# A hybrid decoder layer: two U steps moved ahead of the gate stage, and v loaded four blocks ahead

## The chip, the cores and the metric

The kernel runs on one core of one Trainium2 chip. Its engines work side by side, each through its own list of instructions in order: TensorE (PE: matmuls; PEld: the loading of weights for them), VectorE (DVE), ScalarE (ACT), GpSimd (POOL) and SyncE (SP), which here only issues DMAs. They wait for one another through semaphores. Data lie in HBM, and DMAs bring them to SBUF, the memory on the chip; matmul results are written to PSUM and read from there. The metric is the device time in microseconds (us); less is better.

## The reference

One decoder layer on 512 tokens of width 1024: two token mixers (gated linear attention and a state-space scan), an output projection, and then PEER, a retrieval of single-neuron experts. All that the change touches is in PEER: for each token and each of 8 heads, 16 of 16,384 experts are chosen by product keys.

```
q = (xt @ w_query).reshape(T, H, 2, PEER_HALF)
s = einsum('thpd,hpkd->thpk', q, sub_keys)
top_s, top_i = lax.top_k(s, K)
...
best_s, best_pos = lax.top_k(cand_s, K)
expert_idx = take_along_axis(cand_i, best_pos, axis=-1)
gate = softmax(best_s, axis=-1)
...
act = einsum('td,ted->te', x_blk, u[i_blk])
hid = gelu(act) * g_blk
out = einsum('te,ted->td', hid, v[i_blk])
```

## The kernel before

The tokens are four tiles of 128. For the last tile the chosen rows of u and v are gathered by indirect DMAs that POOL issues: 128 gathers from u, each followed by a product and sum on VectorE, then 128 from v, each added to the output tile (tile n2a). Three buffers (tile gat) take the gathers in turn.

For the other three tiles (384 tokens) all 16,384 experts are computed as matrix products, in 128 blocks of 128 experts. A **U step** multiplies one block of u with the tokens (8 parts of 3 matmuls of 384 columns), and gelu of it is kept in a ring of 59 blocks (tile ring). A **V step** multiplies a block of the ring, which by then also holds the gate of each expert for each token, with a block of v (18 matmuls of 512 columns, into six PSUM tiles that add up all 128 blocks). To keep precision in the fast matmul format, each operand is split in two: the high half is a copy on ACT (uh, vh, hh), the low half is the source minus it, on VectorE or POOL (ul, vl, hl), and three matmuls are made of each product.

The stages, in order: the mixers; the queries and scores; the choice of experts (functions ties, select, gates, spread), with U steps in between; the **gate stage**, in which 48 units of eight tokens each build the matrix of gates (function gunit, matmuls of line 1184 from tiles A and B that gprep makes on VectorE), multiply it into the ring and store the rest to HBM (tile stage, six stores), with U steps spread over the units; four U steps; then a loop over the 128 blocks of v, in which a U step runs beside each of the first 69 V steps, and the last 59 V steps run alone; at the end the final norm.

What sets the order: it is written out by hand, and each engine's list follows the program. select(t) finds the chosen experts of tile t on VectorE (line 974: for each of two halves a comparison, a product, three halving adds and a last add into tile ii), spread(t) transposes ii and the gates on TensorE (lines 1014 to 1016) with one copy on ACT (gs), and spread2(t) copies the rest out of PSUM on VectorE. u_run(n) makes n U steps. Outside the gate stage the lower halves of u are made on POOL, within it and behind it on VectorE (line 104). The number of U steps in the gate stage is what is left: at line 1213, 8 * (59 - 4 - those done) parts, spread evenly over 48 units.

A Stream holds a few raw buffers (tiles ur for u and w_query, vr for v) and three pairs of split halves. Its loads(n) issues the DMAs on SP up to block n, and its split(n) makes the halves up to half n. A load into a raw buffer waits for the split of the block that had the buffer. In the loop, vs.loads(e + 2) stands at the start of step e; the halves of block e + 1 are split in step e, the first of them together with hh and hl of block e + 1 (hprep). The load of a ring block from HBM (gload) stands behind that.

Of the kernel before, what the change touches and what calls it, by code (L numbers as in the profile page):

```python
# [18 lines left out]
D = 1024  # L19
# [44 lines left out]
class Layer:  # L64
# [791 lines left out]
    def experts(self):  # L856
# [117 lines left out]
        def select(t):  # L974

            while any(p[0] == t for p in pieces):
                piece()
            ii = kp.tile([128, 2, 8, 16], F32, name="ii", bufs=2)
            for e in range(2):
                oh = c.tile([128, 8, 16, 16], F16, name="gat", tag="gat", bufs=3)  # L980
                tt(oh, bc(CF[0][:, e, t], 2, 16), bc(itj if e else its, 1, 8), OP.is_equal if e else OP.is_ge)
                tt(oh, oh, TIE[t][:, e], OP.mult)
                for n in (8, 4, 2):
                    tt(oh[:, :, 0:n, :], oh[:, :, 0:n, :], oh[:, :, n:2 * n, :], OP.add)
                tt(ii[:, e], oh[:, :, 0, :], oh[:, :, 1, :], OP.add)
            IX[t] = ii
# [74 lines left out]
        def u_run(n):  # L1061
            for _ in range(n):
                for i in range(8):
                    u_part(i)
# [38 lines left out]
        spread2(0)  # L1103
        spread2(1)
        select(3)
        u_run(3)
        spread(2)
        spread2(2)
        idx = c.tile([128, 128], I32, name="idx")
        gt0 = c.tile([128, 128], F32, name="gt0")  # L1110
# [112 lines left out]
        release()  # L1223
        gctx.close()
        vp = ctx.enter_context(tc.tile_pool(name="vp", bufs=1, reuse_waits="tile"))
        vs = Stream(self, vp, "v", [a["v"][e * 128:(e + 1) * 128, :] for e in range(NE)], 2)
        u_run(LEFT - 1)
        vs.loads(1)
        u_run(1)
        vs.split(1)  # L1230
        hprep(0)

# [16 lines left out]
        def final():  # L1249

            nv = lambda: c.tile([128, 4], F32, name="rs3", bufs=4)
            hf = [slice(0, 512), slice(512, 1024)]
            junk = [c.tile([128, D], F32, name="gat", tag="gat", bufs=3), vp.tile([128, D], F32, name="vr", bufs=2)]
            v = [nv() for _ in range(4)]

            def products(t):
                s = slice(t * 128, t * 128 + 128)
                for n in range(2):
                    for e in (NE - 2, NE - 1):
                        self.mm3(pv[t][n], HT[e][0][:, s], HT[e][1][:, s], *vs.parts[2 * e + n], False, e == NE - 1)  # L1260

            def residual(t, n):
                h = hs[t][:, hf[n]]
                stt(h, pv[t][n], 1.0 / SC, h, OP.mult, OP.add)
                square(t, n)

            def square(t, n):
                act(junk[t % 2][:, hf[n]], hs[t][:, hf[n]], AF.Square, accum_out=v[t][:, n:n + 1])

            def weight(t, n, eng):  # L1270
                eng.tensor_tensor(hs[t][:, hf[n]], hs[t][:, hf[n]], wf[:, hf[n]], op=OP.mult)

            def mean(t):
                V.tensor_scalar(v[t][:, 2:3], v[t][:, 0:1], EPS * D, None, op0=OP.add)
                V.tensor_scalar(v[t][:, 0:1], v[t][:, 1:2], v[t][:, 2:3], 1.0 / D, op0=OP.add, op1=OP.mult)

            def power(t):
                G.tensor_tensor(v[t][:, 3:4], v[t][:, 0:1], self.mhalf, op=OP.pow)

            def scale(t):  # L1280
                stt(hs[t], hs[t], v[t][:, 3:4], wf, OP.mult, OP.mult)
                load(self.out[t], hs[t])

            square(3, 0)
            square(3, 1)
            mean(3)
            power(3)
            for t in range(3):
                products(t)
            residual(0, 0)  # L1290
            residual(0, 1)
            scale(3)
            mean(0)
            power(0)
            residual(1, 0)
            weight(1, 0, G)
            residual(1, 1)
            weight(1, 1, G)
            scale(0)
            mean(1)  # L1300
            power(1)
            residual(2, 0)
            weight(2, 0, G)
            residual(2, 1)
            weight(2, 1, V)
            act(hs[1], hs[1], AF.Copy, scale=v[1][:, 3:4])
            load(self.out[1], hs[1])
            mean(2)
            power(2)
            act(hs[2][:, hf[0]], hs[2][:, hf[0]], AF.Copy, scale=v[2][:, 3:4])  # L1310
            V.tensor_scalar(hs[2][:, hf[1]], hs[2][:, hf[1]], v[2][:, 3:4], None, op0=OP.mult)
            load(self.out[2], hs[2])

        for e in range(NE):
            todo = [gather] * (plan[e + 1] - plan[e])
            pos = [(2 * i + 1) * 7 // max(1, 2 * len(todo)) for i in range(len(todo))]

            def fill(i, todo=todo, pos=pos):
                while pos and pos[0] <= i:
                    pos.pop(0)  # L1320
                    todo.pop(0)()

            vs.loads(e + 2)
            if e == NE - 2:

                hprep(e + 1)
                vs.split(2 * e + 2)
                vs.pair = us.pair
                vs.split(2 * e + 3)
                final()  # L1330
                break
            hh, hl = HT.pop(e)

            def vgrp(n, t):
                s = slice(t * 128, t * 128 + 128)
                vh, vl = vs.parts[2 * e + n]
                self.mm3(pv[t][n], hh[:, s], hl[:, s], vh, vl, e == 0, e == NE - 1)

            for i in range(3):
                vgrp(0, i)  # L1340
                if i == 2:
                    vs.parts.pop(2 * e)
                    vs.split(2 * e + 2)
                    hprep(e + 1)
                    gload(e + 1 + RS)
                u_part(i)
                fill(i)
            u_part(3)
            for i in range(3):
                vgrp(1, i)  # L1350
                if i == 2:
                    vs.parts.pop(2 * e + 1)
                    vs.split(2 * e + 3)
                u_part(4 + i)
                fill(3 + i)
            u_part(7)
            fill(6)
            if e == NE - 12:
                for t in (0, 1):
                    hs[t] = us.c.tile([128, D], F32, name="ur", bufs=2)  # L1360
                    load(hs[t], self.hd[t])
            if e == NE - 4:
                while ng[0] < 256 or pend:
                    gather()
                vs.loads(NE - 1)
                wf = c.tile([128, D], F32, name="gat", tag="gat", bufs=3)
                load(wf, a["w_norm_final"].to_broadcast([128, D]))
                hs[2] = c.tile([128, D], F32, name="gat", tag="gat", bufs=3)
                load(hs[2], self.hd[2])
                hs[3] = acc[0]  # L1370
# [90 lines left out]
```

## Time and profile before

| | us |
|---|---|
| median of 3 runs | 1549.36 |
| lowest, highest | 1544.23, 1552.86 |
| the profiled execution | 1548.65 |
| its span, first to last instruction | 1546.9 |
| TensorE busy | 1490.6 (96%) |
| VectorE busy | 1163.7 (75%) |
| ACT busy | 629.8 (41%) |
| POOL busy | 443.9 (29%) |
| HBM read, written | 315.79 MB, 18.28 MB |

The profile is one execution; its times are counted from the first instruction. Busy shares are means over stages with different limits, so the rows further down go stage by stage. A matmul's end is modelled: two that follow each other overlap in the record, and their pace is read from start to start. DMA share is the mean busy share of the core's 16 DMA engines. The granted clock of TensorE is given as a share of full speed (1.00 is 2.4 GHz, 0.50 is 1.2 GHz). A row's bracket says how long the engine had been idle before it and what ended that.

### The profile page before, as it was taken

How to read it: one execution, taken by the hardware profiler on the slowest of the kernel's cores; microseconds unless marked ns; L12 is line 12 of the kernel's file. 1: busy time of each engine (PE TensorE's matmuls, PEld its weight loads, DVE VectorE, ACT ScalarE, POOL GpSimd, SP SyncE). 2: the span in 40 equal slices, each digit the busy share in tenths (PEclk: the TensorE clock that was granted, in tenths of full speed). 3: DMA queues.
4: the chain of work that ended last, by engine and by line, in shares of the span. 5: the costliest groups of instructions: out<-in, count | busy, mean ns of one | idle time of the engine just before them, and what ended most of it. 6: DMA issues, size and time to landing. Idle time of an engine off the chain costs nothing.

```text
span 1546.9 us, 22385 instructions
## 1 busy us (share of the span) xinstructions
PE 1490.6 (96%) x7904; PEld 1293.0 (84%) x7904; DVE 1163.7 (75%) x2482; ACT 629.8 (41%) x1202; POOL 443.9 (29%) x374
## 2 busy tenths in 40 slices
PE   7999999999888999999999999999999999999997
PEld 6777768888888988889998989999989997777875
DVE  6543554689998999977777777777877776776876
ACT  5445533433644544443333333333333333333433
POOL 1003303444560000002333333333323332333332
PEclk9999999999998999999999999999999999999999
DMA  5231204222233766578888888888998977777885
GB/s 183 89 116 55 95 28 160 86 82 96 90 129 110 191 201 184 168 226 293 305 308 302 295 316 302 312 306 309 315 309 299 318 269 277 249 282 254 294 289 184
DMA packets 148738, 335.56 MB, mean 217 GB/s; under 512 B 64640, under 2 KB 73872, under 8 KB 148496
## 3 DMA queue, kind: packets, MB, share of 16 engines
q1 hardware_dynamic: 58672, 186.32, 35.5%
q0 software_dynamic: 36864, 134.23, 24.1%
q10 hardware_dynamic: 53088, 13.57, 3.8%
q8 instruction: 62, 1.02, 0.3%
q14 instruction: 52, 0.43, 0.1%
HBM read 315.79 MB, written 18.28 MB: 216 GB/s over the span
## 4 chain that ended last, share of the span: by engine, by line
PE 66%; DVE 14%; issue 8%; DMA 8%; ACT 2%; POOL 1%; DVEq 0%; POOLq 0%; SPq 0%; ACTq 0%
PE pm L109 20%; PE pm L108 20%; PE pm L110 20%; DMA gat<-in_v,idx 5%; DVE gat L97 3%; DMA vr<-in_v 2%; PE pg L1184 2%; DVE B L97 1%; POOL gat L1133 1%; DVE ul L104 1%; DVE eq L97 1%; PE pm L902 1%; DVE A L97 1%; DVE ring L97 1%; DVE n2a L100 1%
## 5 line engine op out<-in xcount | busy, mean ns | idle before, releaser
L108 PE MATMUL pm<-nT,uh 128*128 128x384 f32 (+1 forms) x1152 | 404.1, 351 | 3.0 <-ACT uh L91 2.5
L110 PE MATMUL pm<-nT,ul 128*128 128x384 f32 (+1 forms) x1152 | 397.5, 345 | 2.4 <-POOL ul L104 2.4
L109 PE MATMUL pm<-nT,uh 128*128 128x384 f32 (+1 forms) x1152 | 399.0, 346 | 0.5 <-DVE nT L97 0.5
L108 PE MATMUL pm<-vh,hh 128*128 128x512 f32 x765 | 302.7, 396 | 11.4 <-ACT hh L91 9.8
L109 PE MATMUL pm<-vl,hh 128*128 128x512 f32 x765 | 303.4, 397 | 0.2 <-DVE vl L104 0.2
L110 PE MATMUL pm<-vh,hl 128*128 128x512 f32 x765 | 303.4, 397 | 0.1
L1133 POOL DMA_INDIRECT gat<-in_u,idx x128 | 137.3, 1072 | 482.6 <-DVE gat L100 467.3
L91 ACT ACTIVATE uh<-ur 128x512 fp32r<-128x512 f32 x288 | 180.5, 629 | 211.8 <-PE pm L109 190.5
L108 PEld LDWEIGHTS pm<-nT,uh 128*128 128x128 f32 x1152 | 218.0, 189 | 28.5 <-ACT uh L91 2.9
L109 PEld LDWEIGHTS pm<-nT,uh 128*128 128x128 f32 x1152 | 217.6, 189 | 25.5 <-DVE nT L97 1.1
L1133 POOL DMA_INDIRECT gat<-in_v,idx x128 | 148.8, 1162 | 283.9 <-DVE n2a L100 258.3
L110 PEld LDWEIGHTS pm<-nT,ul 128*128 128x128 f32 x1152 | 217.9, 189 | 9.5 <-POOL ul L104 3.6
L91 ACT ACTIVATE vh<-vr 128x512 fp32r<-128x512 f32 x255 | 158.6, 624 | 157.7 <-DMA vr<-in_v 103.1
L104 DVE TENSOR_TENSOR vl<-vr,vh 128x512 fp32r<-128x512 f32 x255 | 174.7, 686 | 62.3 <-ACT vh L91 62.0
L104 DVE TENSOR_TENSOR ul<-ur,uh 128x512 fp32r<-128x512 f32 x212 | 144.5, 689 | 62.4 <-ACT uh L91 61.7
L110 PEld LDWEIGHTS pm<-vh,hl 128*128 128x128 f32 x765 | 144.0, 188 | 36.1 <-DVE hl L104 3.7
L100 DVE SCALAR_TENSOR_TENSOR n2a<-gat,dots,n2a 128x1024 f32<-128x1024 f32 x128 | 163.6, 1278 | 10.0 <-DMA gat<-in_v,idx 6.9
L108 PEld LDWEIGHTS pm<-vh,hh 128*128 128x128 f32 x765 | 144.6, 189 | 29.6 <-ACT hh L91 14.7
L109 PEld LDWEIGHTS pm<-vl,hh 128*128 128x128 f32 x765 | 144.2, 189 | 16.0 <-DVE vl L104 0.5
L100 DVE SCALAR_TENSOR_TENSOR gat<-gat,n2a 128x1024 f32<-128x1024 f32 x128 | 155.9, 1218 | 1.6 <-DMA gat<-in_u,idx 1.6
L91 ACT ACTIVATE gl<-pm 128x384 f32<-128x384 f32 (+17 forms) x107 | 47.4, 443 | 226.3 <-PE pm L110 226.3
L104 POOL TENSOR_TENSOR ul<-ur,uh 128x512 fp32r<-128x512 f32 x76 | 108.7, 1437 | 95.4 <-ACT uh L91 95.1
(254 smaller groups left out, 1705.3 us busy)
## 6 DMA issues: line engine op xcount, KB each, us to landing
ur<-in_uT SPq DMA_DIRECT2D x128, 512.0 KB, 5.8
vr<-in_v SPq DMA_DIRECT2D x128, 512.0 KB, 4.4
gd<-stage ACTq DMA_DIRECT2D x6, 2208.0 KB, 16.1
ring<-gd SPq DMA_DIRECT2D x69, 192.0 KB, 4.7
wraw<-in_w_in SPq DMA_DIRECT2D x23, 512.0 KB, 4.4
ur<-in_w_query SPq DMA_DIRECT2D x16, 512.0 KB, 3.7
b<-in_x SPq DMA_DIRECT2D x8, 512.0 KB, 3.8
wraw<-in_w_out SPq DMA_DIRECT2D x8, 512.0 KB, 3.8
```

The lines of the kernel that those rows point to most:

```text
L91: return self.S.activation(out, in_, f, **k)
L97: return self.V.tensor_tensor(out, x, y, op=op)
L100: return self.V.scalar_tensor_tensor(out, x, s, y, op0=op0, op1=op1, **k)
L104: (self.G if pool else self.V).tensor_tensor(lo, src, hi.bitcast(F32), op=OP.subtract)
L108: T.matmul(out, lhi, rhi, start=start, stop=False)
L109: T.matmul(out, lhi, rlo, start=False, stop=False)
L110: T.matmul(out, llo, rhi, start=False, stop=stop)
L902: T.matmul(p[:, t * 128:(t + 1) * 128], q[:, t * 128:(t + 1) * 128], skT[:, b, :], start=True, stop=True)
L1133: G.indirect_dma_start(out=r, out_offset=None, in_=src, in_offset=bass.IndirectOffsetOnAxis(ap=idx[:, k:k + 1], axis=0))
L1184: T.matmul(o, A[:, t // 2, :, t % 2], B[:, i, t // 2, :, t % 2], start=i == 0, stop=i == 1)
```

## The change

Two edits. In the choice of experts, the three U steps between select(3) and spread(2) become two, and three new ones stand behind spread(2); since the gate stage takes what is left, it has 32 U steps instead of 34. For v, the stream has four raw buffers instead of two, two more loads stand ahead of the loop, and the loop issues the load of block e + 4. The fifth changed line only names the new number of buffers where the final norm borrows one.

```
         select(3)
+        u_run(2)
+        spread(2)
         u_run(3)
-        spread(2)
         spread2(2)
...
-        vs = Stream(self, vp, "v", [a["v"][e * 128:(e + 1) * 128, :] for e in range(NE)], 2)
+        vs = Stream(self, vp, "v", [a["v"][e * 128:(e + 1) * 128, :] for e in range(NE)], 4)
         u_run(LEFT - 1)
         vs.loads(1)
         u_run(1)
+        vs.loads(3)
         vs.split(1)
...
-            junk = [c.tile([128, D], F32, name="gat", tag="gat", bufs=3), vp.tile([128, D], F32, name="vr", bufs=2)]
+            junk = [c.tile([128, D], F32, name="gat", tag="gat", bufs=3), vp.tile([128, D], F32, name="vr", bufs=4)]
...
-            vs.loads(e + 2)
+            vs.loads(e + 4)
```

On ACT at the end of the choice of experts, one U step is two splits (uh from ur) and one gelu into the ring (ring from pm); gs is the copy of spread(2), and the rows from pg are the first unit of the gate stage:

```order
 L91 ACTIVATE uh<-ur 128x512 x2
 L91 ACTIVATE ring<-pm 128x384
-L91 ACTIVATE uh<-ur 128x512 x2
-L91 ACTIVATE ring<-pm 128x384
 L91 ACTIVATE gs<-pm 128x128
-L91 ACTIVATE ring<-pg 128x38x8
-L91 ACTIVATE stage<-pg 128x69x8
-L91 ACTIVATE uh<-ur 128x512 x2
-L91 ACTIVATE ring<-pg 128x38x8
+L91 ACTIVATE uh<-ur 128x512 x2
+L91 ACTIVATE ring<-pm 128x384
```

The copy moves ahead of one U step, and three U steps (the first of them in the last two rows) stand between it and the first unit.

On POOL at the same place stand the lower halves of u, then the gathers of u:

```order
 L104 TENSOR_TENSOR ul<-ur,uh 128x512 x2
 L881 IOTA its 128x128
-L104 TENSOR_TENSOR ul<-ur,uh 128x512 x46
-L1133 DMA gat<-in_u,idx 128x1024 x128
...
+L104 TENSOR_TENSOR ul<-ur,uh 128x512 x50
+L1134 DMA gat<-in_u,idx 128x1024 x128
```

Four splits more stand ahead of the first gather.

On SP, from the last selection to the first step of the loop over v (ur is a block of u, vr one of v, ring one of the stored gates):

```order
-L88 DMA ur<-in_uT 128x1024 x17
+L88 DMA ur<-in_uT 128x1024 x19
 L88 DMA n2a<-n2d 128x1024
-L88 DMA ur<-in_uT 128x1024 x37
+L88 DMA ur<-in_uT 128x1024 x35
 L88 DMA vr<-in_v 128x1024 x2
 L88 DMA ur<-in_uT 128x1024
+L88 DMA vr<-in_v 128x1024 x2
 L88 DMA ring<-gd 128x384
 L88 DMA vr<-in_v 128x1024
```

Two loads of u move ahead of the load of n2a, and two loads of v ahead of the first ring block; each later v load keeps its place in the list and brings a block two further on.

## Rows read from the trace of the kernel before

**Rows 1.** Stretches: length, busy us of each engine (instructions), PEclk, DMA share, GB/s.
```profile
core 0: us, PE busy (x) PEld busy (x) DVE busy (x) ACT busy (x) POOL busy (x), PEclk, DMA share, GB/s
...
457.90:468.40 10.50, 0.05 (x1) 0.00 (x0) 10.09 (x20) 0.42 (x2) 1.96 (x3) 0.64 0.19 59
468.40:512.00 43.60, 43.19 (x348) 41.45 (x348) 38.34 (x72) 21.41 (x49) 1.79 (x2) 0.93 0.51 150
512.00:672.00 160.00, 151.89 (x1234) 142.49 (x1232) 158.32 (x284) 74.24 (x181) 10.32 (x9) 1.00 0.61 179
...
691.90:1276.30 584.40, 584.27 (x2899) 526.32 (x2899) 449.15 (x707) 212.97 (x412) 186.98 (x175) 1.00 0.87 303
1276.30:1537.50 261.20, 251.60 (x1063) 200.24 (x1062) 193.21 (x256) 98.50 (x187) 87.81 (x72) 0.99 0.75 264
```

**Rows 2.** Groups, 1276.3 to 1537.5: count | busy us, mean ns | idle before, releasers.
```profile
L108 PE MATMUL pm<-vh,hh 128*128 128x512 f32 x351 | 139.0, 396 | 9.4 <-ACT hh L91 7.8 <-ACT vh L91 1.5
...
L100 DVE SCALAR_TENSOR_TENSOR n2a<-gat,dots,n2a 128x1024 f32<-128x1024 f32 x71 | 90.7, 1278 | 2.2 <-DMA gat<-in_v,idx 2.0
...
L91 ACT ACTIVATE vh<-vr 128x512 fp32r<-128x512 f32 x115 | 71.9, 628 | 156.0 <-DMA vr<-in_v 103.1 <-PE pm L110 49.8 <-DVE n2a L100 3.0
```

**Rows 3.** PE in order of time: start us, us, what, [idle before <-releaser].
```profile
1000.24 0.40 PE L108 MATMUL pm<-vh,hh 128*128 128x512 f32 x1
...
1000.71 0.40 PE L110 MATMUL pm<-vh,hl 128*128 128x512 f32 x1
...
1416.35 0.39 PE L110 MATMUL pm<-vh,hl 128*128 128x512 f32 x1
1418.67 0.50 PE L108 MATMUL pm<-vh,hh 128*128 128x512 f32 x1 [1.94 <-ACT hh L91]
...
1424.13 0.39 PE L108 MATMUL pm<-vh,hh 128*128 128x512 f32 x1
...
1433.65 0.39 PE L108 MATMUL pm<-vh,hh 128*128 128x512 f32 x1
```

**Rows 4.** SP's queue and ACT in order of time, around one pause.
```profile
1410.33 0.33 SPq L88 DMA_DIRECT2D vr<-in_v  x1
...
1417.57 0.63 ACT L91 ACTIVATE vh<-vr 128x512 fp32r<-128x512 f32 x1 [6.11 <-DMA vr<-in_v]
```

**Rows 5.** ACT in order of time: the gelus of two U steps in a row.
```profile
453.50 0.49 ACT L91 ACTIVATE ring<-pm 128x384 f32<-128x384 f32 x1 [1.56 <-PE pm L110]
...
457.66 0.49 ACT L91 ACTIVATE ring<-pm 128x384 f32<-128x384 f32 x1 [1.56 <-PE pm L110]
```

**Rows 6.** PE in order of time: spread(2) and the first gate matmul.
```profile
457.46 0.27 PE L1014 MATMUL pm<-ident,ii 128*128 128x128 f32 x1
...
468.44 0.29 PE L1184 MATMUL pg<-B,A 128*128 128x128 f16 x1 [10.49 <-DVE B L97]
```

**Rows 7.** DVE in order of time: start and end of select(2) and of select(3).
```profile
438.34 2.32 DVE L97 TENSOR_TENSOR gat<-tops,its 128x2048 f16<-128x2048 f16 x1
...
451.10 3.44 DVE L97 TENSOR_TENSOR gat<-gat 128x1024 f16<-128x1024 f16 x3
454.57 0.29 DVE L97 TENSOR_TENSOR ii<-gat 128x128 f32<-128x128 f16 x1
...
455.97 1.21 DVE L97 TENSOR_TENSOR gat<-tops,its 128x2048 f16<-128x2048 f16 x1
...
463.66 1.47 DVE L97 TENSOR_TENSOR gat<-gat 128x1024 f16<-128x1024 f16 x3
465.17 0.29 DVE L97 TENSOR_TENSOR ii<-gat 128x128 f32<-128x128 f16 x1
```

**Rows 8.** POOL in order of time, beside select(2) and select(3).
```profile
450.43 3.50 POOL L104 TENSOR_TENSOR ul<-ur,uh 128x512 fp32r<-128x512 f32 x2 [0.45 <-ACT uh L91]
454.59 1.42 POOL L104 TENSOR_TENSOR ul<-ur,uh 128x512 fp32r<-128x512 f32 x1 [0.66 <-ACT uh L91]
456.18 2.14 POOL L104 TENSOR_TENSOR ul<-ur,uh 128x512 fp32r<-128x512 f32 x1 [0.17 <-ACT uh L91]
466.55 1.47 POOL L1133 DMA_INDIRECT gat<-in_u,idx  x1 [8.23 <-DVE idx L100]
```

**Rows 9.** Groups on DVE, 468.4 to 672: the splits of u.
```profile
L104 DVE TENSOR_TENSOR ul<-ur,uh 128x512 fp32r<-128x512 f32 x67 | 44.4, 682 | 5.1 <-ACT uh L91 4.7
```

**Rows 10.** POOL's gathers, 1276 to 1500: from issue to landing.
```profile
DMA to landing us min/median/max: 4.7/6.2/8.4
```

## The prediction

> **What bounds the kernel now.** I read first the table of stages [rows 1], then inside one stage the groups of instructions [rows 2], and last the order in time around single pauses. The table cuts the second half of the kernel into five stretches. From 468.4 to 672 us the gate matrices are built and spread: VectorE is busy 158.3 of 160.0 us between 512 and 672, so it is the bound there, and what is taken from TensorE in that stretch brings nothing by itself. From 691.9 to 1276.3 us a U step and a V step alternate: TensorE is busy 584.3 of 584.4 us, nothing waits. Two stretches are different. From 457.9 to 468.4 us TensorE stands still, 10.5 us. And from 1276.3 to 1537.5 us only V steps are left: 59 of them, 1,062 matmuls of 512 columns, and they take 261.2 us.
>
> What should those 59 steps take? In a clean piece of the same stage 42 matmuls lie between 1424.13 and 1433.65 us [rows 3]: 9.52 / 42 = 0.2267 us each. 1,062 of them are 240.8 us. So the stage loses **20.4 us**. The groups name who ends the pauses: TensorE waits for ACT's hh, which stands in ACT's queue behind vh, and vh is what waits for the load of v, 103.1 us in the stage [rows 2]. One pause in full: the load is issued at 1410.33, vh can start at 1417.57 after 6.11 us of idle ACT [rows 4], and TensorE's next matmul comes at 1418.67 after 1.94 us of idle [rows 3]. The load took 7.1 us. With two raw buffers it can't be issued before the block two back is split, about one and a half steps (1.5 x 4.08 = 6.1 us) before its own split is due. The engines are not full: DMA share 0.75 at 264 GB/s here against 0.87 at 303 GB/s in the stage before [rows 1]. So it is a matter of when the load starts, not of bandwidth. The recorded waits of TensorE add up to only 9.4 us [rows 2] of the 20.4, because matmul ends are modelled (0.39 us each where 0.2267 us passes to the next start) and because the granted clock dips behind a pause.
>
> **Part one: four raw buffers, loads four steps ahead.** No instruction is added; 128 loads stay 128. In the V stage the load of block e+4 goes out where that of e+2 did, with the same wait (the split of the block that had the buffer). It now has about 3.5 x 4.08 = 14 us to land against the 7.1 of the bad case. ACT's wait for v goes to about nothing, and with it the 20.4 us. What is late next? VectorE needs 1.28 us for each of 71 gathers' sums [rows 2] and three splits a step; it sits idle 68 of 261 us [rows 1], so it has room. A denser stage moves its bytes in less time: the share rises from 0.75 to about 0.75 x 261 / 245 = 0.80. In the alternating stage, at 0.87, the same V matmul is 0.235 us apart (1000.24 to 1000.71, two matmuls) instead of 0.2267 [rows 3]. Going (0.80 - 0.75) / (0.87 - 0.75) = 0.42 of that way costs 0.42 x 0.0083 x 1,062 = 3.7 us. A late gather may cost about 1 us more. Bounds: all 20.4 back; or the whole 0.0083 us for every matmul, 8.8 us, leaving 11.6. I take 20.4 - 3.7 - 1.0 = **15.7 us gained**, nearer to the upper end, since the share stays nearer to today's.
>
> The two extra loads ahead of the loop are queued on SP behind the last U load and before the first ring load. The ring load waited there anyway for VectorE's first split of h, and is read 59 steps later. The fourth v load waits for the last store of the stage tiles, which the ring load also waited for. I cost that at nothing; if the 1 MB delayed the U load before it, it would be 2 x 512 KB at 300 GB/s, 3.5 us, once.
>
> **Part two: the U steps.** Three U steps stood before the last selection transposes, none behind; now two stand before and three behind. Two U steps so come out of the gate stage (34 steps there become 32) into the 10.5 us hole. A U step is 4.16 us of TensorE (457.66 - 453.50, the ends of two of them on ACT) [rows 5]. Line by line:
>
> TensorE first. Its two steps before the transposes end at 457.46 - 4.16 = 453.3 [rows 6]; but the transposes read what select(2) writes, and that is done at 454.57 + 0.29 = 454.86 [rows 7]. So it waits 1.6 us, which the slack behind it covers. The three steps then run to about 455.3 + 12.5 = 467.8, almost to 468.44, where the first gate matmul starts today [rows 6]. The hole would be filled exactly, if VectorE kept its time.
>
> It doesn't. Every U step has two splits, and in this stretch their lower halves run on POOL. Four more of them (46 in one row become 50) now run beside select(3). The rows show what that costs: select(2), with POOL at work (3.50 us for two splits) [rows 8], takes from 438.34 to 454.86, 16.5 us; the same instructions of select(3), mostly with POOL silent until its first gather at 466.55, take from 455.97 to 465.46, 9.5 us. Three adds are 3.44 us in the one and 1.47 us in the other [rows 7]. With POOL at work to about 468, select(3) does 12.0 / 16.5 = 73% of itself by then and the remaining 27% at the quiet pace (some 2.3 us): end at 470.3, **4.9 us later**. Everything behind it on VectorE (spread2(2), idx, the first A, eq and B) and with it the first gate matmul is 4.9 us later. Bounds: nothing, if the splits slip between; 7.0 us, if all of select(3) goes at the pace of select(2).
>
> The Trainium skill, "SBUF — State Buffer", section "Who interferes with whom", has the rule for it: a VectorE instruction with two SBUF inputs and a GpSimd instruction that reads SBUF exclude each other, and the later one blocks. By that rule, with 1.42 us for a split beside little work [rows 8], four splits would hold VectorE up to 5.7 us instead of 4.9, and the end would be 0.8 us later than below; the trace agrees in direction (3.44 against 1.47 us).
>
> Against it, the gate stage: VectorE is its bound, and it loses four lower halves that POOL now does. 67 of them take 44.4 us there [rows 9], 0.66 us each: 2.7 us. The ring products take in two more of the finished blocks from the first unit on, and two separate gelu products fall away; both are parts of a microsecond and I count them even. TensorE loses 8.3 us of work there, which shortens only units where it is the later one. I take 2.7 us, the lower end; 8.3 is the upper. The granted clock is 0.64 in the hole and 0.93 after it [rows 1], so 7% of 43.6 us, 3 us of work, is lost at the lower level. TensorE will still stand from 467.8 to about 473.3, so I count nothing back. Sum of part two: +4.9 - 2.7 = **2.2 us lost**, between 8.3 gained and 7.0 - 2.7 = 4.3 lost.
>
> **The sum.** The profiled run took 1548.65 us (span 1546.9), the median of three is 1549.36, so no correction: 1548.65 - 15.7 + 2.2 = 1535.15, given as **1535 us**.
>
> **Rivals.**
> Gathers take over (slower). Three gather buffers go round: landing, then 1.28 us of sum, then the next issue. The stage has 71 sums in its first 54 steps, 71 / 3 = 23.7 rounds. At TensorE's pace these steps are 54 x 4.08 = 220 us, 9.3 us a round, so a mean landing over 8.0 us begins to hold VectorE, whose queue then holds the splits of v. At today's pace (54 x 261.2 / 59 = 239 us, 10.1 a round) break-even is 8.8. The landings are 4.7 / 6.2 / 8.4 us [rows 10]. At 9.5 us the 54 steps take 23.7 x 10.8 = 256 us, the stage 276 instead of 261: 1548.65 + 15 + 2.2 = 1566. It speaks for it that loads that no longer wait lie on the same DMA engines; against it that the alternating stage has 175 POOL issues in 584.4 us, one in 3.3 us, at 303 GB/s, and TensorE loses nothing. Chance 0.06.
>
> The Trainium skill, "DMA: Bandwidth & Descriptors", section "Issuing engines are not separate DMA queues", says that transfers issued by different engines run on the same 16 engines and interleave; by it the earlier v loads can lengthen a gather's landing, which is this rival's start, and no run here shows yet by how much.
>
> Only the recorded waits come back (no change). Then 9.4 us is the gain, the rest of the 20.4 being slower pace that stays, and part two costs its upper end: 1548.65 - 9.4 + 4.3 = 1543.6. For it: the lost time is larger than any row names. Against: the pause of 1.94 us is 2.3 us from start to start (1416.35 to 1418.67 [rows 3]), and the dips come behind pauses. Chance 0.20.
>
> The loads do not run ahead. If SP's queue, in order, held the loads until the old time, the gain would be nothing and the time 1548.65 + 2.2 = 1551. Against: in the V stage v loads are alone in that queue. Chance 0.05.
>
> **How the numbers follow.** The forecast has 0.69. Its own ends are 1548.65 - 20.4 - 8.3 = 1520 and 1548.65 - 11.6 + 4.3 = 1541.4, the lower one not likely with both at once. For 8 in 10 I give 1526 to 1545, which takes in the second rival. Half a percent, about what a measurement of this kernel can tell from no change, is 7.7 us: faster means under 1541.6, slower over 1557.1. Faster: 0.66, the forecast without its upper edge. Within: 0.27 (edge, second and third rival). Slower: 0.07.
>
> **What would show it.** Right: ACT's wait for v in the V stage from 103 us to under 15; 59 steps in 242 to 250 us; TensorE without waits for hh; DMA share there about 0.80. For part two: three U steps behind the transposes, select(3) lasting 13 to 16 us, the first gate matmul near 473 us, gate units to about 674. Wrong: VectorE waiting for gathers by tens of us (first rival); V stage over 252 us with no v wait left (second); v waits as today (third); select(3) still 9.5 us, which would make part two a gain of 2.7 us or more.

## The result

The changed kernel took **1526.86 us** (median of 4 executions, 1523.84 to 1533.17) against 1547.09 for the kernel before, measured beside it (4, 1544.23 to 1552.86): ratio **0.987, 95% interval 0.982 to 0.992**. Measured again on another chip, ten executions gave 1532.39 (1525.79 to 1536.14) against 1539.02 (19, 1527.57 to 1552.54): 0.9947, 0.991 to 0.9984. So it is faster, by 1.3% in the one set and by 0.5% in the other; how much depends on two things that vary from one execution of the same kernel to the next, and which the experiments below separate.

The profiled execution took 1524.62 us (span 1522.8), 24.0 us under that of before. The stretches of after, with the columns of [rows 1]; the boundaries are the first gate matmul (473.6), the end of the gate units (674.4 and what is left of U to 695.3), the last U matmul (1272.4):

```profile
core 0: us, PE busy (x) PEld busy (x) DVE busy (x) ACT busy (x) POOL busy (x), PEclk, DMA share, GB/s
...
468.10:473.60 5.50, 0.05 (x1) 0.00 (x0) 5.29 (x13) 0.49 (x1) 2.44 (x3) 0.81 0.33 108
473.60:512.00 38.40, 38.00 (x311) 36.41 (x312) 35.17 (x65) 19.06 (x45) 1.80 (x2) 0.94 0.46 143
512.00:674.40 162.40, 149.60 (x1221) 138.54 (x1220) 158.86 (x285) 72.89 (x178) 10.29 (x9) 1.00 0.61 176
...
695.30:1272.40 577.10, 575.83 (x2899) 521.05 (x2900) 449.54 (x707) 212.76 (x413) 187.87 (x175) 1.00 0.88 308
1272.40:1514.30 241.90, 241.45 (x1063) 199.07 (x1061) 194.46 (x259) 101.68 (x187) 84.16 (x71) 1.00 0.82 281
```

Against [rows 1]: V steps begin 3.4 us later (695.3, before 691.9), the alternating stage is 7.3 us shorter (577.1, before 584.4), the V-only stage 19.3 us shorter (241.9, before 261.2), and the tail behind it 0.9 us shorter (8.5, before 9.4). 3.4 - 7.3 - 19.3 - 0.9 = -24.1, which is the difference.

The V-only stage of after by groups (1272.4 to 1514.3), which answers to [rows 2]:

```profile
L108 PE MATMUL pm<-vh,hh 128*128 128x512 f32 x351 | 136.7, 389 | 0.2 <-ACT vh L91 0.2
L100 DVE SCALAR_TENSOR_TENSOR n2a<-gat,dots,n2a 128x1024 f32<-128x1024 f32 x71 | 90.8, 1280 | 3.2 <-DMA gat<-in_v,idx 3.2
...
L91 ACT ACTIVATE vh<-vr 128x512 fp32r<-128x512 f32 x115 | 72.8, 633 | 135.1 <-PE pm L110 133.7 <-DVE vl L104 1.4
```

ACT's idle time ahead of vh has not gone (135.1 us, before 156.0), but its releaser has changed: 133.7 us of it now end with TensorE giving back a buffer of split halves, and the load of v, 103.1 us before, is not in the list. TensorE's idle time ahead of this matmul fell from 9.4 to 0.2 us. TensorE is now the bound, and ACT waits for it.

PE of after in order of time, the stretch that answers to [rows 3]; 42 matmuls lie between the two lines:

```profile
1423.99 0.39 PE L108 MATMUL pm<-vh,hh 128*128 128x512 f32 x1
...
1433.51 0.39 PE L108 MATMUL pm<-vh,hh 128*128 128x512 f32 x1
```

9.52 / 42 = 0.2267 us, the pace of the clean piece of before, though the DMA share of the stage has risen from 0.75 to 0.82.

The choice of experts in after, VectorE first (select(3) starts with the first line; [rows 7] has it before), then POOL ([rows 8]), then PE at spread(2) and at the first gate matmul ([rows 6]):

```profile
456.27 1.22 DVE L97 TENSOR_TENSOR gat<-tops,its 128x2048 f16<-128x2048 f16 x1
457.52 2.19 DVE L97 TENSOR_TENSOR gat<-gat,k 128x2048 f16<-128x2048 f16 x1
459.75 4.40 DVE L97 TENSOR_TENSOR gat<-gat 128x1024 f16<-128x1024 f16 x3
...
467.89 2.43 DVE L97 TENSOR_TENSOR gat<-gat 128x1024 f16<-128x1024 f16 x3
470.36 0.29 DVE L97 TENSOR_TENSOR ii<-gat 128x128 f32<-128x128 f16 x1
```

```profile
456.57 7.44 POOL L104 TENSOR_TENSOR ul<-ur,uh 128x512 fp32r<-128x512 f32 x4 [2.34 <-ACT uh L91]
465.29 3.69 POOL L104 TENSOR_TENSOR ul<-ur,uh 128x512 fp32r<-128x512 f32 x2 [1.28 <-ACT uh L91]
```

```profile
455.22 0.33 PE L1015 MATMUL pm<-ident,ii 128*128 128x128 f32 x1 [1.31 <-DVE ii L97]
...
473.64 0.29 PE L1185 MATMUL pg<-B,A 128*128 128x128 f16 x1 [5.49 <-DVE B L97]
```

TensorE waits 1.31 us for select(2) and 5.49 us before the gates, where it was 10.49 us in one piece. But the second pause ends 5.20 us later (473.64, before 468.44), since select(3), 9.5 us before, now takes 470.36 + 0.29 - 456.27 = 14.4 us beside six splits on POOL, where one lay beside it before.

### The profile page after: what moved, and what is told of

Read it like the earlier page. It is cut to its first block, busy times and chain, and to the rows that moved or that the text cites. A ratio compares the mean times of both kernels' runs of the same rounds, so it can differ in the third digit from the quotient of the medians.

```text
span 1522.8 us, 22405 instructions
## 1 busy us (share of the span) xinstructions
PE 1473.2 (97%) x7904; PEld 1284.2 (84%) x7904; DVE 1166.3 (77%) x2476; ACT 632.5 (42%) x1200; POOL 449.4 (30%) x378
## 3 DMA queue, kind: packets, MB, share of 16 engines
q8 instruction: 62, 1.02, 0.3%
## 4 chain that ended last, share of the span: by engine, by line
PE 77%; DVE 14%; DMA 3%; issue 3%; ACT 2%; POOL 0%; SPq 0%; DVEq 0%; ACTq 0%; POOLq 0%
PE pm L109 24%; PE pm L110 24%; PE pm L108 24%; DVE gat L97 3%; DVE ul L104 2%; DMA gd<-stage 1%; DVE B L97 1%; PE pg L1185 1%; DVE eq L97 1%; DVE A L97 1%; DVE ring L97 1%; DMA ur<-in_uT 1%; PE pm L902 1%; DVE gat L100 1%; ACT b L91 1%
## 5 line engine op out<-in xcount | busy, mean ns | idle before, releaser
L108 PE MATMUL pm<-vh,hh 128*128 128x512 f32 x765 | 298.9, 391 | 2.3 <-ACT hh L91 2.0
L1134 POOL DMA_INDIRECT gat<-in_u,idx x128 | 137.1, 1071 | 471.1 <-DVE gat L100 461.3
L108 PEld LDWEIGHTS pm<-vh,hh 128*128 128x128 f32 x765 | 143.9, 188 | 16.7 <-ACT hh L91 2.3
L100 DVE SCALAR_TENSOR_TENSOR gat<-gat,n2a 128x1024 f32<-128x1024 f32 x128 | 156.0, 1218 | 1.7 <-DMA gat<-in_u,idx 1.6
L104 POOL TENSOR_TENSOR ul<-ur,uh 128x512 fp32r<-128x512 f32 x80 | 116.2, 1460 | 98.4 <-ACT uh L91 98.2
L91 ACT ACTIVATE gl<-pm 128x384 f32<-128x384 f32 (+16 forms) x105 | 46.5, 443 | 222.7 <-PE pm L110 136.8
```

Of the source, the lines that this page charges most:

```text
L91: return self.S.activation(out, in_, f, **k)
L100: return self.V.scalar_tensor_tensor(out, x, s, y, op0=op0, op1=op1, **k)
L104: (self.G if pool else self.V).tensor_tensor(lo, src, hi.bitcast(F32), op=OP.subtract)
L108: T.matmul(out, lhi, rhi, start=start, stop=False)
L1134: G.indirect_dma_start(out=r, out_offset=None, in_=src, in_offset=bass.IndirectOffsetOnAxis(ap=idx[:, k:k + 1], axis=0))
```

## The experiments

Twelve more runs were made, two of them of kernels that had been run already (before and after, again) and two of one and the same new kernel (h first). Each run left one trace. The table reads four starts in each trace: the first gate matmul, the first V matmul, the last U matmul, the last V matmul. "Alternating" is from the second to the third, "V only" from the third to the fourth; those are starts, so they lie within 1 us of the stretches above. The ratio is to the kernel before, timed beside each kernel on the same chip; it is taken over the executions and need not be the quotient of two medians.

| kernel | buffers | first gate | first V | alternating | V only | profiled us | ratio to before |
|---|---|---|---|---|---|---|---|
| before | 2 | 468.4 | 691.9 | 584.2 | 260.3 | 1548.65 | |
| after | 4 | 473.6 | 695.4 | 576.8 | 241.1 | 1524.62 | 0.987 |
| v parts alone | 4 | 469.6 | 692.7 | 578.4 | 241.1 | 1523.34 | 0.9946 |
| U steps alone | 2 | 472.2 | 694.9 | 584.2 | 257.8 | 1548.41 | 1.0064 |
| buffers alone | 4 | 469.9 | 692.8 | 575.2 | 241.1 | 1520.57 | 0.993 |
| three buffers | 3 | 470.2 | 693.4 | 584.0 | 241.1 | 1530.15 | 0.989 |
| before, again | 2 | 471.1 | 694.2 | 583.8 | 253.0 | 1542.49 | 0.9979 |
| after, again | 4 | 473.6 | 695.1 | 586.6 | 241.1 | 1534.14 | 0.9947 |
| h first | 3 | 469.8 | 692.5 | 574.4 | 241.1 | 1519.60 | 0.9862 |
| no gathers | 4 | 473.0 | 682.9 | 585.1 | 241.1 | 1520.66 | 0.9841 |
| half loads | 2 | 471.0 | 694.2 | 575.9 | 242.1 | 1523.72 | 0.9899 |
| h first, U moved | 3 | 472.9 | 694.8 | 576.0 | 241.1 | 1523.50 | 0.9894 |
| h first, again | 3 | 465.7 | 689.3 | 576.0 | 241.1 | 1517.98 | 0.9866 |
| gathers late | 3 | 468.4 | 682.5 | 582.7 | 241.1 | 1517.94 | 0.9838 |

### The parts of the change, one at a time

The v parts alone: the changed kernel, with the U steps as before.

```
-        u_run(2)
-        spread(2)
         u_run(3)
+        spread(2)
         spread2(2)
```

> Part one alone: four raw buffers for v, loads four blocks ahead, U steps as before. If the parts add as the two traces read (V stage 261.2 to 241.9 us from part one; first gate matmul 5.2 us later, gate stage's end 2.4 us later from part two), this kernel is 2 to 3 us faster than both edits together and about 20 us faster than before: V stage 241 to 244 us, first gate matmul at 468.4, gate stage's end at 671 to 672. The rival, that part two gains by itself and the two traces only hide it, expects this kernel slower than both edits together. The stretch of alternating U and V steps: if its 7.4 us belong to the edit, 577 us here and 584 in the next kernel; if they are the run's, no such order.

Median 1530.79 (1522.5 to 1534.46), ratio 0.9946 (0.9915 to 0.9977). The V-only stage is that of after to 0.1 us: this part alone brings all of it.

The U steps alone: the kernel before, with the reverse of that edit.

> Part two alone: two U steps before the last transposes and three behind, v as before. My working: first gate matmul at 473.3 to 473.7 (5 us late), gate stage's end 2 to 3 us late, V stage 261 us as before: 1 to 3 us slower than before. Rival, the hole was worth filling: 3 us or more faster. Alternating stretch 584 us if its length belongs to the v edit.

Median 1548.89 (1539.86 to 1555.56), ratio 1.0064 (1.003 to 1.0098): a loss, and with 9.9 us more than the 1 to 3 us expected. The gate stage starts at 472.2 and V at 694.9, as in after. V so starts 3.0 us later than in the first trace of before; the rest of the 9.9 us is not in this trace, whose alternating stage is as long (584.2) and whose V-only stage is 2.5 us shorter (257.8). With two buffers that stage varies from one execution to the next, as shown below; whether the moved U steps lengthen it stays open.

The buffers alone, against the v parts alone:

```
-        vs.loads(3)
...
-            vs.loads(e + 4)
+            vs.loads(e + 2)
```

> Four raw buffers, but the loads still written where they were (block e + 2 at step e, no loads ahead of the loop), U steps as before. If the lead comes from the buffers (in the V stage SP's list holds only v loads, each waits only for its buffer, so SP runs ahead by itself), ACT's wait for v falls from 103 us to under 15 and the V stage to 241 to 246 us, as in part one. If the place in the program gives the lead, the V stage stays at 258 to 262 us.

Median 1530.25 (1517.52 to 1533.58), ratio 0.993 (0.9891 to 0.997), V only 241.1. The place of the issue in the program makes no difference: in the V-only stage SP has little else in its queue and runs ahead on its own; what held a load was the buffer.

Three buffers, loads three steps ahead, against the v parts alone:

```
-        vs = Stream(self, vp, "v", [a["v"][e * 128:(e + 1) * 128, :] for e in range(NE)], 4)
+        vs = Stream(self, vp, "v", [a["v"][e * 128:(e + 1) * 128, :] for e in range(NE)], 3)
...
-        vs.loads(3)
+        vs.loads(2)
...
-            vs.loads(e + 4)
+            vs.loads(e + 3)
```

> Three raw buffers, loads three blocks ahead, U steps as before. Lead: about 2.5 steps, 10 us, against landings that reached 7.1 us: V stage 241 to 245 us, the whole gain of 19 us with half the added memory. If the loads' lateness were a matter of bandwidth or of bursts that a longer lead only spreads, a third buffer brings half: V stage about 250 us.

Median 1522.0 (1516.85 to 1531.54), ratio 0.989 (0.9857 to 0.9923), V only 241.1. One buffer more is enough; the fourth buys nothing.

### What varies between executions of one kernel

The kernel before and the changed kernel once more, with no edit.

> The kernel before once more. It asks two things. First, how long its alternating U/V stage takes when it is drawn again: in the traces so far that stage ran at one of two steady paces, about 325 matmuls in 65 us (584 us in all: before, and the two runs with part two alone and with three buffers) or about 330 (575 to 578 us: after, part one alone, four buffers alone). If the pace is drawn anew in every execution, this trace can show 584 or 576, with the rest as in the trace of before; if the two raw buffers set the slow pace, it shows 584 again, and the executions with three buffers at 584 speak against that already. Second, the V-only stage: 258 to 262 us with the wait of ScalarE for the raw v in both theories. Ratio to the kernel before: 1.000, within 0.003 either way.

> The changed kernel on the same chip as the others of this set. If the two parts add up, it stands at the product of their ratios, 0.9946 by 1.0064 = 1.001 (0.995 to 1.006); if part two costs only the 2 to 3 us that its own stage shows, it stands at 0.996 or below. V stage 242 us, gate units end about 4.5 us later than in part one alone, first V step about 695 us.

Median of before again 1544.11 (1528.46 to 1554.56), ratio 0.9979 (0.9932 to 1.0026), so no difference, as it must be. But its V-only stage took 253.0 us where the first trace of before has 260.3, with the same list of waits (groups of the second trace of before, 1278.2 to 1532):

```profile
L108 PE MATMUL pm<-vh,hh 128*128 128x512 f32 x351 | 137.9, 393 | 4.9 <-ACT hh L91 4.0 <-ACT vh L91 1.0
L91 ACT ACTIVATE vh<-vr 128x512 fp32r<-128x512 f32 x115 | 72.4, 630 | 149.4 <-DMA vr<-in_v 101.5 <-PE pm L110 39.2 <-DVE n2a L100 6.4
```

With two buffers this stage comes out at 253.0, 257.8 and 260.3 in three traces; with three or four it is 241.1 in all ten. The change gains **12 to 19 us** here, and takes away a spread.

The second trace of after is 9.5 us longer than the first, and nearly all of it is the alternating stage (586.6, against 576.8). In the same stretch, 830 to 895 us, first of after, then of after again:

```profile
830.00:895.00 65.00, 65.00 (x331) 58.88 (x330) 50.04 (x87) 24.79 (x48) 21.02 (x20) 1.00 0.88 307
```

```profile
830.00:895.00 65.00, 65.00 (x325) 58.63 (x324) 49.08 (x85) 24.03 (x47) 20.47 (x20) 1.00 0.87 301
```

331 matmuls or 325 in 65 us, TensorE without a pause and at full granted clock in both. The stage runs at one of these two paces from its first steps to its last: seven traces have it at 574.4 to 578.4 us, seven at 582.7 to 586.6.

The ratio of after again, 0.9947 (0.991 to 0.9984), is that of the v parts alone (0.9946). It lies with the second case, in which part two costs 2 to 3 us (0.996 or below), and not at the 1.001 that the cost of 0.64% would give; but its interval overlaps the 0.995 to 1.006 of that case, so the larger cost is made unlikely and not excluded. The pair of runs with h first, below, prices part two better.

### Does the DMA load or VectorE set the pace?

The changed kernel without gathers:

```
-                G.indirect_dma_start(out=r, out_offset=None, in_=src,
-                                     in_offset=bass.IndirectOffsetOnAxis(ap=idx[:, k:k + 1], axis=0))
...
-                stt(r, r, 1.0, n2, OP.mult, OP.mult, accum_out=dots[:, k:k + 1])
+                if j == 0:
+                    V.memset(dots, 0.5)
...
-                stt(acc[0], r, gw[:, k:k + 1], acc[0], OP.mult, OP.add)
+                pass
```

> The changed kernel without the 256 gathers of rows of u and v and without VectorE's 256 products on them: the dots are a constant, and the token that is computed from the gathered rows comes out as nothing but its first addend. It measures what the gathers' transfers (512 KB each) and VectorE's work on them cost TensorE's pace. If the pace of the V matmuls falls with the DMA share, as the prediction's 3.7 us held, the V-only stage goes to about 240.8 us at 0.2267 us a matmul (from 241.9, where it is already), and the alternating stage, whose share falls from 0.88 to about 0.7, gains 10 to 20 us over 577. If the pace does not hang on the DMA share, the V-only stage keeps 0.227 to 0.2275 us a matmul, and the alternating stage shows 575 to 585 us, at one of its two paces.

The stretches of this kernel, alternating and V only:

```profile
682.90:1268.30 585.40, 584.29 (x2899) 526.39 (x2900) 246.14 (x414) 212.44 (x412) 0.00 (x0) 1.00 0.45 149
1268.30:1510.30 242.00, 241.53 (x1063) 199.09 (x1061) 114.19 (x188) 101.57 (x187) 2.79 (x3) 1.00 0.39 129
```

The DMA share is halved (0.45 for 0.88, 0.39 for 0.82) and VectorE's work nearly so, and the alternating stage shows its longer time, no other than at full share (585.1 us, with gathers 582.7 to 586.6), the V-only stage the same 242.0 us. So neither pace hangs on the DMA share or on VectorE, and the gathers are not on the path of the V-only stage. What the gathers do cost lies in the gate stage: V starts at 682.9, 12.4 us sooner than in after.

### Is it the turn of two buffers?

Before, with two buffers, but every load of v half as long:

```
+            if s.nm == "v":
+                s.y.load(s.raw[s.nl][:, 0:512], s.src[s.nl][:, 0:512])
...
-            s.y.split(hi, lo, s.raw[i][:, k * 512:(k + 1) * 512], pool)
+            w = 0 if s.nm == "v" else k
+            s.y.split(hi, lo, s.raw[i][:, w * 512:(w + 1) * 512], pool)
```

> The kernel before, two raw buffers, but each load of v brings only the first half of its rows (256 KB in place of 512) and both splits of the step read that half, so the second half of every product with v is that of the first. If the V-only stage of before is bound by the turn of two buffers (a load can start only when its buffer is read out, and then takes its whole landing time), halving the landing time alone brings the stage to 241 to 243 us, ScalarE's wait for v to under 15 us, with two buffers. If something else holds it, it stays at 253 to 261. It also asks whether two buffers go with the slow pace of the alternating stage: if so, that stage shows 584 and the executions lie on one level; if the pace is drawn anew in each execution, they lie on two levels some 8 us apart, as those of the kernels with three and four buffers do (1523 and 1531).

Groups of its V-only stage (1270.3 to 1513.2; lines are four higher than in before):

```profile
L112 PE MATMUL pm<-vh,hh 128*128 128x512 f32 x351 | 136.7, 389 | 0.2 <-ACT vh L95 0.2
L95 ACT ACTIVATE vh<-vr 128x512 fp32r<-128x512 f32 x115 | 72.6, 632 | 137.2 <-PE pm L114 90.8 <-DMA vr<-in_v 43.4 <-DVE vl L108 1.4
```

The stage takes 242.1 us, TensorE's idle is 0.2: with a shorter load two buffers do. So the lost time was the landing time of a load that starts too late; that it is not the bytes is shown by three buffers, which bring the same bytes without the loss. I was wrong on the wait: ACT still waits 43.4 us for v, not under 15, but no longer so late that TensorE notices; a wait on ACT is a loss only when it is the last. The alternating stage drew the shorter time (575.9), so two buffers by themselves don't force the longer one (with whole loads they have shown no other, in three traces), and executions lie at 1523.72, 1524.25, 1527.46, 1531.84 and 1532.34, with one between the two levels.

### The memory of hl, and the price of part two

In after, VectorE's first hl waited for the last store of the gate stage, and TensorE 1.20 us for hl (DVE, then PE, in order of time):

```profile
696.69 0.56 DVE L104 TENSOR_TENSOR hl<-ring,hh 128x384 fp32r<-128x384 f32 x1 [0.97 <-DMA gd<-stage]
```

```profile
697.30 0.79 PE L110 MATMUL pm<-vh,hl 128*128 128x512 f32 x1 [1.20 <-DVE hl L104]
```

The pool of v is opened where that of the gate stage was closed, so with more raw buffers hl may come to lie on a store buffer. To move it, three buffers and this edit, U steps as before:

```
-            HT[e] = [vp.tile([128, TD], F32R, name=n, bufs=2) for n in ("hh", "hl")]
+            if e:
+                HT[e] = [vp.tile([128, TD], F32R, name=n, bufs=2) for n in ("hh", "hl")]
...
+        HT[0] = [vp.tile([128, TD], F32R, name=n, bufs=2) for n in ("hh", "hl")]
         vs = Stream(self, vp, "v", [a["v"][e * 128:(e + 1) * 128, :] for e in range(NE)], 3)
```

> Three raw buffers, loads three steps ahead, the U steps as before, and the memory of the first hidden tile's high and low parts (hh, hl) taken ahead of the raw buffers of v. If the first V step is late because hl lies on the gate stage's second store buffer, whose store runs until about 696 us, the wait of VectorE for that store goes at hl, and V starts at 691 to 692 us in place of 693.4; then the raw buffers lie where hl lay, and it is the third or fourth load of v that waits, which nobody needs yet. If the placement has nothing to do with it, V starts at 693 to 694 us. V-only stage 241 to 243 us in both. Time: 0 to 2 us under the version with three buffers (ratio 0.989 there, 0.985 to 0.992 here).

Median 1519.23 (1518.46 to 1529.2), ratio 0.9862 (0.9785 to 0.9939). V starts at 692.5, within what the others show without it (691.9 to 694.2). The trace of three buffers without this edit has no such wait either, so the edit had nothing to take away: the run does not test the placement. The wait stands in all five traces with four raw buffers (0.9 to 2.0 us on TensorE) and in none of the nine with two or three. So it goes with the number of buffers; that the placement makes it is argued, not shown.

The same kernel with part two and without, on one chip:

> Three raw buffers with the hidden tile's memory taken first, and part two of the change with it: the price of part two alone, against the same kernel without it in this set. By the traces (first V step 2.3 to 3 us later with part two: 694.9, 695.4 and 695.1 against 692.7, 692.8 and 693.4) it is 2 to 3 us slower than that kernel, ratio 1.0015 to 1.002 between the two; by the ratio of part two alone to the kernel before (1.0064) it is 5 to 15 us slower; by the ratios of the changed kernel and of part one alone (0.9947, 0.9946) there is no difference. V stage 241 to 242 us, first gate matmul at 472 to 474 us.

> Three raw buffers with the hidden tile's memory taken first, U steps as before, timed again at more rounds for the comparison with part two. Ratio to the kernel before 0.983 to 0.990; executions on two levels, 1519 and 1528 us, by the pace of the alternating stage.

With it 1524.72 (1523.5 to 1534.28; ratio 0.9894, 0.9856 to 0.9932), without it 1520.85 (1517.98 to 1530.62; ratio 0.9866, 0.9828 to 0.9904). Each has four executions on a lower and two on an upper level, with medians 1524.3 and 1534.1 against 1519.6 and 1529.7. Between like and like part two costs 4.7 and 4.5 us, by these few executions. The traces say where some of it is, as means of the four traces with part two (after, after again, U steps alone, this one) and the eight others that keep the gathers in place: first gate matmul at 473.1 against 469.5 us (+3.6), from there to the end of the last gate matmul 199.5 against 201.8 (-2.3), from there to the first V matmul 22.4 against 21.3 (+1.1); together 2.4 us later. The last of the three was not in the prediction. The first gate matmul varies by itself from 465.7 to 471.1 in the eight, so 2.4 and 4.6 are not apart.

### A version that beats both

Without gathers, the gate stage ended 11 us sooner than in after. So three buffers, h first, U steps as before, and:

```
-            if u % 4 == 3:
-                gather()
```

> The same kernel with the 12 gathers of the gate stage left to the alternating stage, whose plan spreads them. Without any gather the gate units ended at 660.5 us in place of 671.6 to 671.9, so VectorE's products and their waits cost the gate stage about 11 us. If the alternating stage, whose VectorE is busy 450 of 577 us, takes 12 more products beside its matmuls, V starts at 681 to 684 us and the whole is 8 to 11 us faster than without this edit, 1508 to 1520 us. If the alternating stage is held up by them (its DMA share is 0.88), the gain is given back there: V stage and gate stage as expected, but 580 to 595 us between them, and no gain.

The gate stage of this kernel and its alternating stage, and under it the same two of the version without the edit (h first, first run):

```profile
468.40:660.00 191.60, 189.31 (x1553) 180.60 (x1553) 184.00 (x332) 94.78 (x227) 1.71 (x2) 0.99 0.56 158
...
682.50:1265.40 582.90, 582.75 (x2899) 525.10 (x2900) 458.57 (x724) 213.09 (x412) 197.10 (x182) 1.00 0.88 310
```

```profile
469.80:670.80 201.00, 192.38 (x1566) 181.20 (x1567) 194.90 (x352) 94.88 (x227) 12.05 (x11) 0.99 0.60 175
...
692.50:1267.10 574.60, 574.46 (x2899) 519.68 (x2900) 450.37 (x707) 213.22 (x412) 188.98 (x175) 1.00 0.88 308
```

VectorE, the bound of the gate stage, does 10.9 us less there, and the stage is 9.4 us shorter. The alternating stage takes 582.9 us, which lies in the 580 to 595 us of the rival. But it shows 325 or 326 matmuls in every 65 us, as the other traces with the longer time do, and no new wait on TensorE; so it is read here as a drawn longer time, and VectorE takes the 8 us of work into its idle time. Median 1520.01 (1511.48 to 1525.21), ratio **0.9838 (0.980 to 0.9875)**, the lowest measured for a kernel that does all the work; but its interval overlaps that of the version without the edit (0.9866), so the gain of 9.4 us is shown in its stage and not in the total.

## Why the prediction came out as it did

Predicted were 1535 us (1526 to 1545) and faster with 0.66; measured were 1526.86, at the lower edge of the range, and faster.

**What bounds the kernel: right.** The V-only stage lost its time to loads that started too late, not to bandwidth: halving the load with two buffers, or a third buffer, brings it to 241 or 242 us. Between the two profiled executions 19.3 of the 20.4 us came back (261.2 to 241.9), not only the 9.4 that the waits recorded. ACT's wait for v left the list. The second rival falls: it needs a stage of some 252 us, and every trace with three or four buffers has 241.1 from start to start.

**The pace term of 3.7 us: wrong, this is the step that failed.** I read the 0.235 us between V matmuls in the alternating stage as the price of its DMA share of 0.87, and put 42% of the way on every V matmul at 0.80. The share went to 0.82, a little more than forecast, and the pace stayed at 0.2267. Without gathers the alternating stage ran at a share of 0.45, and its V matmuls were still 0.23 to 0.24 us apart (PE of that kernel in order of time):

```profile
1000.64 0.40 PE L108 MATMUL pm<-vh,hh 128*128 128x512 f32 x1
1000.88 0.40 PE L109 MATMUL pm<-vl,hh 128*128 128x512 f32 x1
1001.11 0.40 PE L110 MATMUL pm<-vh,hl 128*128 128x512 f32 x1
```

(1001.11 - 1000.64) / 2 = 0.235. Some of the difference was the longer of the two paces, which the first trace of before had drawn: the median over the stage, from one V matmul to the V matmul behind it, is 0.234 us in before and without gathers, but 0.232 in after, at a share of 0.88. The rest does not follow the DMA share either; what sets it is open. Two stages that differ in DMA share differ in other things too. The term measures nothing.

**The late gather, 1.0 us: nothing.** The V-only stage is 242.0 us without gathers and 241.9 with them; 1,063 x 0.2267 = 241.0 is all but the whole of it. In after VectorE waits 3.2 us in all for gathers (the groups above), TensorE not at all. The first rival, gathers that take over, has nothing for it. Without these two terms the sum of the prediction is 1548.65 - 20.4 + 2.2 = 1530.5.

**The alternating stage, counted as unchanged: right as a mechanism, and still 7.4 us of the profiled difference.** The change doesn't touch it; the first trace of before had its longer time, the first of after its shorter. I made the sum against one execution as if that were the kernel. 1530.5 - 7.4 = 1523.1, and 1524.62 was measured in that execution. By the second traces the parts are 253.0 and 241.1 in the V-only stage, 583.8 and 586.6 in the alternating one: 8.35 us of gain in all (1542.49 to 1534.14).

**That the size came near is in part luck.** The prediction gave part one 15.7 us. From the three traces with two buffers and whole loads (260.3, 257.8 and 253.0 us) to 241.1 us the gain is 19.2, 16.7 and 11.9 us, 15.9 in the mean. The 20.4 us were read from the longest of the three and stand 4.5 us above that mean, and the two terms that measure nothing took off 4.7. Of the 13.5 us forecast in all (15.7 less 2.2) the two sets gave 20.2 us (1547.09 to 1526.86) and 6.6 (1539.02 to 1532.39), one above and one below.

**Two extra loads ahead of the loop, at nothing: right.** With the v parts alone the time from the end of the last gate matmul to the first V matmul is 21.3 us, as before. But a wait that the prediction had not named came with four buffers, TensorE's 0.9 to 2.0 us for hl.

**Part two, 2.2 us lost: right by its own steps.** The transposes were predicted to wait 1.6 us for select(2), and waited 1.31. The end of select(3) was predicted at 470.3 and seen at 470.65; of the sum behind it, 27% of 9.5 us are 2.6 us and not 2.3, so the working itself gives 470.6. The first gate matmul was predicted at 473.3 and seen at 473.64. The gate stage was to become 2.7 us shorter. Its last unit, in before and then in after, in PE's order of time:

```profile
669.41 1.17 PE L1184 MATMUL pg<-B,A 128*128 128x128 f16 x16
```

```profile
671.94 1.02 PE L1185 MATMUL pg<-B,A 128*128 128x128 f16 x15 [0.36 <-DVE B L97]
```

From the first gate matmul to the end of the last it took 669.41 + 1.17 - 468.44 = 202.1 us, and now takes 671.94 + 1.02 - 473.64 = 199.3: 2.8 us less, and 2.3 over all traces. VectorE did 63 lower halves there (473.6 to 674.4), where [rows 9] has 67. Left out was the 1.1 us between the gate units and V; where it comes from is open. The net loss is 2.4 us by the traces and some 4.6 by the executions with three buffers, where the upper bound was 4.3. Alone, with two buffers, it measured 9.9, and what stands above the bound there is not explained.

The rule of the Trainium skill ("SBUF — State Buffer", section "Who interferes with whom"), by which I had the end up to 0.8 us later, agrees in direction: three halving adds took 4.40 us beside POOL, and 1.47 alone. select(3) lasted 14.4 us where my rows gave 14.3 and the rule up to 15.1. Both were worked out for four more splits beside it, and it was five (six, before one).

**The loads do not run ahead: falls.** The V-only stage is 241.1 us in ten traces, and even with the issue at its old place.

## What to carry to other kernels

Where a stage waits on loads while the DMA engines have room, count how long a load may take between the release of its buffer and its own use; one buffer more was worth 12 to 19 us, a second one and an earlier issue nothing. Filling an idle hole of one engine with work whose helper instructions fall beside the critical instructions of another makes the hole end later: two U steps put in a 10.5 us hole of TensorE lost 2.4 to 4.7 us, and alone, with two buffers, 9.9. Before a small term is read from two stages of one trace, ask what else differs between them, and profile the kernel before a second time: its V-only stage alone moved by 7 us.

## What the runs showed of the hardware

- The alternating stage runs at one of two steady paces in each trace, 325 or 331 matmuls in 65 us, about 8 us in all, at a granted clock of 1.00 and without pauses. It is not the DMA share (longer at 0.45, shorter at 0.83), not VectorE's load (longer with 246 us of it, shorter with 450), not part two (seen at both). Nor is it the number of buffers alone: three and four have been seen at both, two with half loads at the shorter, and two with whole loads, in three traces, only at the longer. What chooses is open. The V-only stage has one pace alone.
- Three halving adds on VectorE in a row, the first 128x1024 f16, took 1.47 us alone, 2.43 us partly beside POOL's splits and 4.40 us beside four of them in a row; the four traces with part two agree (4.39 or 4.40, and 2.43 or 2.44).
- After the pause of 5.49 us before the gates the granted clock of the next 38.4 us was 0.94, after the pause of 10.49 us in before 0.92: half the pause gave back 0.02 x 38.4 = 0.8 us of full clock.
